# A chunk's and a state's products, put side by side on TensorE in the SSD part of a hybrid decoder layer

## The chip, the cores and the metric

The kernel runs on one core of a Trainium2 chip. The metric is the device time of one execution in microseconds. Three runs of the kernel before took 2318.2, 2318.97 and 2319.44 us; their median, 2318.97, is the time before.

## The reference

One inference step of a decoder layer: half a SwiGLU step, a mixer, half a SwiGLU step, each with a residual sum and an RMS norm ahead of it, and a last norm. 1024 positions of a prompt and 8 samples with 4 positions each go through the same weights (1056 columns in all). The mixer projects into two groups of heads, S5 and SSD. The change touches the SSD group: 24 heads of 64 in 4 groups of B and C, state of 128, chunks of 128 positions.

```python
acum = jnp.cumsum(la, axis=2)                       # la = dt * a, inside a chunk
decay = jnp.exp(jnp.where(mask, diff, -jnp.inf))    # diff[l, s] = acum[l] - acum[s]
cb = jnp.einsum('bclgn,bcsgn->bclsg', cm, bm)
y_diag = jnp.einsum('bclsg,bclsgr,bcsgrp->bclgrp', cb, decay, xd)
states = jnp.einsum('bclgn,bclgr,bclgrp->bcgrpn', bm, dstate, xd)
def step(hc, inp):
    st, dec = inp
    return hc * dec[..., None, None] + st, hc       # h_enter: the state ahead of each chunk
y_off = jnp.einsum('bclgn,bcgrpn,bclgr->bclgrp', cm, h_enter, jnp.exp(acum))
ys = (y_diag + y_off + d * xh) * silu(z)            # then a grouped RMS norm over 384 channels
```

The prompt has 8 chunks that hand a state on. Each of the 8 samples brings a state of its own (`h0`) into one short chunk of 4 positions; all 8 samples' positions lie in one block of 32 columns, called chunk 8 in the kernel.

## The kernel before

All heavy products are done with fp32 values split into two halves, so that a product is three matmuls: high by high, high by low, low by high. The 1056 columns are cut into three blocks of 352. `dense` (L301) runs over blocks and contraction tiles; one step of it, a `unit`, is the three matmuls of L317, L318 and L319 on one block, and after it `tick` (L192) is called.

**The order of the work is written out by ticks.** Whatever lies beside the dense products is put into queues with `later(gap, fn, q)` (L189). At every tick, `tick` issues the stores and the calls that `at(n, fn)` has set for this tick, then steps each queue: the first entry runs when at least `gap` ticks have passed since the queue's last step. An entry may be a generator; each `yield n` puts its rest back with gap n. Engines execute their own instructions in the order in which this program issues them, and wait for each other by semaphores. So a gap sets after how many dense units the instructions stand in each engine's queue, and not when they run.

**The SSD part** lies beside dense products: group 0 beside the projections of group 1 (`group(g)`, L1373, 8 tiles of 24 units), group 1 beside those of group 2, and so on; group 3 runs beside the output projections (`out`, L2020). `ssd_steps(g)` (L1700) gives `steps`, which queues nine rounds, i = 0 to 8, for chunks in the order 8, 0, 1, ..., 7:

- `stage_a(c)` (L1723). VectorE and ScalarE make the decay matrices (`dec`), ScalarE `ce`; after `a_dec` and `a_exp` ticks TensorE makes C by B and the transposes of B and x (L1743 to L1746), and the sums of the squares of an earlier chunk (`y_sums`, L1788); after `a_pe` VectorE makes `xd` and `xds`; after `a_mul` VectorE multiplies `dec`, and GpSimd `ce`.
- `stage_b(c)` (L1792), one round behind `stage_a`. TensorE makes the chunk's output into one bank (L1802: 12 products, 64 columns of stationary each, two of which lie side by side; 6 for chunk 0) and the new state into another (L1803). After `b_pe` VectorE adds the state up (`hT`) and GpSimd decays it (`hS`); after `b_y`, `y_done` (L1772) has VectorE make the gated output `yf`, ScalarE its square, and GpSimd two sums over the three channel tiles. The sums over the partitions are left to the next `y_sums`.
- `sample_h(b)` (L1839), the work on sample b's state: the store of the state before, the load of the state two ahead (after `sample` ticks), six products of the state (L1847, 64 columns of stationary and 4 streamed), one product for its update (L1848, 128 columns of stationary, 384 streamed), GpSimd's decay of the state, and after `add` ticks VectorE's two sums. `sample_b` (L1823) makes the output of the samples' block itself (L1828, once for a group, in round 1).

`sample_done` (L1860) ends a group: the sums of the last `y_done`, then the samples' `y_done`, then its sums. The last chunk's `stage_b(7)`, its sums and the row of norms are `tail` steps in round 0 of the next group. Four PSUM banks go round for these steps (`abank`, L246): two in `stage_a`, two in `stage_b`, one in `sample_h`. Buffers of `stage_a` (`prod`) are two deep, `xb` and the states three, `yf` one.

The gaps are in `GAP` (L36). Before the change a round is: `a` ticks, `stage_a`, `b` ticks, `stage_b`, `h` ticks, `sample_h`, with 4, 2 and 4 (in group 3: 4, 2 and 8), `first` and `second` in place of `a` in rounds 0 and 1.

Of the kernel before, what the change touches and what calls it, by code (L numbers as in the profile page):

```python
# [33 lines left out]
ADD, SUB, MUL = ALU.add, ALU.subtract, ALU.mult  # L34

GAP = dict(  # L36
    rs=14, rs1=1, rs2=1, a=4, b=2, h=4, a3=4, b3=2, h3=8, first=7, second=6, tail0=4, tail1=10, tail2=5, done=6, done2=6, done3=6, done4=6, add=4,
    a_dec=1, a_exp=2, a_pe=2, a_mul=2, b_pe=2, b_y=1, load_a=3, sample=6, split=18, split2=18, split_hi=5, split_lo=2, v0=1,
    v1=6, v2=6, v3=3, glu1=5, glu2=11, low=5, load=14, t0=12, t1=16, u0=8, u1=12, v_0=7, v_1=14, out=16, zout=2, s5z=6, row=4, s5a=6,
    s5b=5, s5c=6, s5d=4, prep=8, tiny=7, table=4,  # L40
# [94 lines left out]
class Build:  # L135
# [1564 lines left out]
    def ssd_steps(self, g):  # L1700
        nc, L, o = self.nc, self.later, self.o
# [70 lines left out]
        def y_done(c, n, x, z, p3, s):  # L1772
            cs = slice(128 * c, 128 * c + n)
            y = self.yf[:, :, 0:n]
            for j in range(3):
                self.stt(y[:, j], x[:, j], self.dcol[:, 3 * g + j:3 * g + j + 1], p3[:, j], MUL, ADD)
            self.tt(y, y, z, MUL)
            self.act(s, y, AF.Square)
            self.store(self.dO[g, :, :, cs].rearrange("j p c -> p j c"), y)
            for j in (1, 2):  # L1780
                self.tt(s[:, 0], s[:, 0], s[:, j], ADD, nc.gpsimd)
            cur["sum"] = (c, n, s[:, 0])

        def y_sums(p):

            if "sum" in cur:
                c, n, s = cur.pop("sum")
                nc.tensor.matmul(p[0:n, 400:401], s, self.ones[:, 0:1], start=True, stop=True)  # L1788
                return lambda: self.ts(self.rv[0:n, c:c + 1], p[0:n, 400:401], 1.0 / 384, MUL, EPS, ADD)
            return lambda: None  # L1790

        def stage_b(c):  # L1792
            xb, (dec, ce, xd, xds, bt) = cur.pop(c)
            z = cur.pop(("z", c))
            p3, p4 = self.abank(), self.abank()
            for j in range(3):
                for off in range(2 if c else 1):
                    for e in range(2):
                        out = p3[64 * e:64 * e + 64, 128 * j:128 * j + 128]
                        r = 2 * j + e  # L1800
                        lhs, rhs = ((xd, dec), (self.hT, ce))[off]
                        nc.tensor.matmul(out, lhs[:, 64 * r:64 * r + 64], rhs[:, r], start=(off == 0), stop=(off == 1 or c == 0))  # L1802
            nc.tensor.matmul(p4[:, 0:384], bt, xds, start=True, stop=True)  # L1803
            yield GAP["b_pe"]
            if c == 0:
                nc.vector.tensor_copy(self.hT, p4[:, 0:384])
            else:
                self.tt(self.hT, self.hS, p4[:, 0:384], ADD)
            if c < 7:
                self.tt(v6(self.hS), v6(self.hT), self.cd[:, c + 1, h6, None].broadcast_to([128, 6, 64]), MUL, nc.gpsimd)  # L1810
            yield GAP["b_y"]
            y_done(c, 128, xb[:, 2:5], z, p3[:, 0:384].rearrange("p (j c) -> p j c", j=3), xd.rearrange("p (j c) -> p j c", j=3))
            self.xb.put(xb)
            self.zg.put(z)
            if c == 7:
                nc.sync.dma_start(o["ssdp"][g], self.hT)

        def sample_load(b):
            h0 = self.h0.get()
            nc.sync.dma_start(h0, self.a["h0"][g, :, b])  # L1820
            cur["h", b] = h0

        def sample_b():  # L1823
            _, (dec, ce, xd, xds, bt) = cur.pop(8)
            p3 = self.abank()
            for r in range(6):
                out = p3[64 * (r % 2):64 * (r % 2) + 64, 32 * (r // 2):32 * (r // 2) + 32]
                nc.tensor.matmul(out, xd[0:32, 64 * r:64 * r + 64], dec[0:32, r, 0:32], start=True, stop=True)  # L1828
            nc.vector.tensor_copy(self.ys, p3[:, 0:96].rearrange("p (j c) -> p j c", j=3))

        def sample_m(b):
            self.ts(self.bm[b % 2], self.bst.bitcast(F32), self.bmask[:, b:b + 1], MUL)

        def sample_out(b):
            h0 = cur.pop(("h", b))
            nc.sync.dma_start(o["ssds"][g, :, b], h0)
            self.h0.put(h0)

        def sample_h(b):  # L1839
            h0, bm, p = cur["h", b], self.bm[b % 2], self.abank()  # L1840
            if b:
                sample_out(b - 1)
            if b + 2 < 8:
                self.at(GAP["sample"], lambda: sample_load(b + 2))
            for r in range(6):
                out = p[64 * (r % 2):64 * (r % 2) + 64, 384 + 4 * (r // 2):388 + 4 * (r // 2)]
                nc.tensor.matmul(out, h0[:, 64 * r:64 * r + 64], self.ces[:, r, 4 * b:4 * b + 4], start=True, stop=True)  # L1847
            nc.tensor.matmul(p[:, 0:384], bm, self.xst, start=True, stop=True)  # L1848
            self.tt(v6(h0), v6(h0), self.cds[:, b, h6, None].broadcast_to([128, 6, 64]), MUL, nc.gpsimd)

            def add():
                y = self.ys[:, :, 4 * b:4 * b + 4]
                self.tt(y, y, p[:, 384:396].rearrange("p (j c) -> p j c", j=3), ADD)
                self.tt(h0, h0, p[:, 0:384], ADD)
                if b < 7:
                    sample_m(b + 1)

            self.at(GAP["add"], add)
# [15 lines left out]
        def steps(nxt=None):  # L1874

            tail, self.tail = self.tail, [
                lambda: stage_b(7),
                lambda: (y_sums(self.abank())(), self.rs_root(self.ry))[1],
                lambda: (self.rs_row(self.ry, self.rsd[2 + g]), self.rs_done.add(g)),
            ]  # L1880
            ga, gb, gh = (GAP[k + ("3" if g == 3 else "")] for k in "abh")
            for i in range(9):
                c = (i + 8) % 9
                L((GAP["first"], GAP["second"])[i] if i < 2 else ga, lambda c=c: stage_a(c))
                if i == 0:
                    for n, fn in enumerate(tail):
                        L(GAP[f"tail{n}"], fn)
                    L(0, lambda: (load_z(8), load_z(0), sample_load(0), sample_load(1), sample_m(0)))
                else:
                    L(gb, sample_b if i == 1 else lambda c=c: stage_b(c - 1))  # L1890
                    if c < 7:
                        L(0, lambda c=c: self.at(6, lambda: load_z(c + 1)))
                    L(gh, lambda b=i - 1: sample_h(b))
            if nxt:
                L(0, nxt)
            L(GAP["done3" if g == 3 else "done"], sample_done)
# [255 lines left out]
```

## Time and profile before

| what | value |
|---|---|
| median of three runs | 2318.97 us |
| the profiled execution | 2322.18 us |
| its span, first to last instruction | 2320.5 us |
| mean granted TensorE clock | 0.993 |
| TensorE matmuls busy | 2277.6 us (98%), 16463 instructions |
| VectorE busy | 1509.0 us (65%) |
| ScalarE busy | 844.0 us (36%) |
| GpSimd busy | 383.0 us (17%) |
| SSD steps in the span | about 947 to 1523 us |

The page gives shares over the whole span, of which the SSD steps take a quarter. The lists in order of time carry the start in us from the span's start, the length, the engine, the line, what is written and read, how many instructions of that kind follow one another, and in square brackets the idle time of the engine ahead of it with what ended it. An fp32 product counts as two matmuls there. PEld is the load of stationaries, which can run under a matmul of the stationary before. Starts of matmuls are what to read; their lengths are modelled and overlap. In the view by stretches each engine has its busy time and number of instructions, then the granted clock, the DMA engines' share and GB/s.

### The profile page before, as it was taken

To read this page: it belongs to the slowest core of one execution; us is meant where nothing else is said; L and a number is where in the kernel's file an instruction comes from. 1 tells how busy PE (TensorE), PEld (TensorE's weight loads), DVE (VectorE), ACT (ScalarE), POOL (GpSimd) and SP (SyncE) were. 2 spreads that over 40 slices of the span, in tenths; PEclk is the share of its full clock that TensorE was granted. 3 is DMA by queue.
4 is the path that set the end of the run, shared out by engine and by line. 5 is a ranking of instruction groups with operands and counts; after the bars stand their busy time and mean duration, and the time that the engine had idled before them with its cause. 6 is when DMAs were issued, how large, how long until landed. Compare 5 with 4: busy or idle time off the path is not lost. (4 is left out here: it accounts for less than half of the span.)

```text
span 2320.5 us, 40946 instructions
## 1 busy us (share of the span) xinstructions
PE 2277.6 (98%) x16463; PEld 2218.2 (96%) x16463; DVE 1509.0 (65%) x3110; ACT 844.0 (36%) x1372; POOL 383.0 (17%) x446
## 2 busy tenths in 40 slices
PE   9999999999999999999999999999999999999997
PEld 9999999999999899999999889999999999999997
DVE  6988887662326377787889788767855555553325
ACT  5433334340113123555555553233433333341122
POOL 1200000000002133242333374422100000000013
PEclk9999999999999999999999999999999999999999
DMA  4222233362311354563555735432222222263112
GB/s 148 84 70 89 102 119 102 120 236 89 102 53 50 118 180 146 154 194 124 173 159 162 226 111 153 145 118 93 87 77 77 74 84 79 85 246 120 61 51 75
DMA packets 191548, 274.68 MB, mean 118 GB/s; under 512 B 31615, under 2 KB 137342, under 8 KB 191358
## 3 DMA queue, kind: packets, MB, share of 16 engines
q1 hardware_dynamic: 190782, 271.54, 35.7%
q8 instruction: 129, 2.11, 0.4%
q10 hardware_dynamic: 576, 0.52, 0.1%
q14 instruction: 61, 0.50, 0.1%
HBM read 195.17 MB, written 76.84 MB: 117 GB/s over the span
## 5 line engine op out<-in xcount | busy, mean ns | idle before, releaser
L317 PE MATMUL b<-xn,ws 128*128 128x352 f32 (+3 forms) x1776 | 595.0, 335 | 5.7 <-DVE tb L145 3.2
L318 PE MATMUL b<-xn,ws 128*128 128x352 f32 (+3 forms) x1776 | 574.9, 324 | 2.3 <-DVE xn L155 2.3
L319 PE MATMUL b<-xn,ws 128*128 128x352 f32 (+3 forms) x1776 | 574.1, 323 | 0.0
L317 PEld LDWEIGHTS b<-xn,ws 128*128 128x128 f32 x1776 | 335.4, 189 | 16.1 <-DVE tb L145 4.1
L318 PEld LDWEIGHTS b<-xn,ws 128*128 128x128 f32 x1776 | 337.4, 190 | 7.1 <-DVE xn L155 2.8
L681 PE MATMUL b<-xn,ws 128*128 128x264 f32 x1184 | 338.3, 286 | 5.8 <-ACT g L158 5.8
L683 PE MATMUL b<-xn,ws 128*128 128x264 f32 x1184 | 339.2, 286 | 2.3 <-DVE ws L145 2.3
L682 PE MATMUL b<-xn,ws 128*128 128x264 f32 x1184 | 338.5, 286 | 0.0
L319 PEld LDWEIGHTS b<-xn,ws 128*128 128x128 f32 x1776 | 335.9, 189 | 0.0
L158 ACT ACTIVATE ws<-wr 128x512 fp32r<-128x512 f32 (+4 forms) x208 | 170.3, 821 | 316.9 <-PE b L318 282.4
L145 DVE TENSOR_TENSOR ws<-wr,ws 128x512 fp32r<-128x512 f32 (+4 forms) x208 | 221.8, 1067 | 80.2 <-ACT ws L158 79.7
L681 PE MATMUL b<-d,ws 128*128 128x264 f32 x888 | 252.9, 285 | 1.0 <-DVE g L145 1.0
L682 PE MATMUL b<-d,ws 128*128 128x264 f32 x888 | 252.9, 285 | 0.0
L683 PE MATMUL b<-d,ws 128*128 128x264 f32 x888 | 252.8, 285 | 0.0
L145 POOL TENSOR_TENSOR acc<-acc,g 128x400 f32<-128x400 f32 (+2 forms) x25 | 37.6, 1503 | 1197.9 <-ACT g L158 1197.6
L155 DVE SCALAR_TENSOR_TENSOR x<-b,x 128x352 f32<-128x352 f32 (+2 forms) x144 | 73.5, 522 | 246.7 <-PE b L319 246.6
L681 PEld LDWEIGHTS b<-xn,ws 128*128 128x128 f32 x1184 | 224.2, 189 | 7.8 <-ACT g L158 7.1
L145 DVE TENSOR_TENSOR g<-b,g 128x264 f32<-128x264 f32 (+1 forms) x311 | 134.1, 432 | 150.1 <-PE b L683 105.1
L683 PEld LDWEIGHTS b<-xn,ws 128*128 128x128 f32 x1184 | 223.9, 189 | 3.1 <-DVE ws L145 3.1
L682 PEld LDWEIGHTS b<-xn,ws 128*128 128x128 f32 x1184 | 223.6, 189 | 0.0
L317 PE MATMUL b<-d,ws 128*128 128x352 f32 (+2 forms) x534 | 172.6, 323 | 0.0
L319 PE MATMUL b<-d,ws 128*128 128x352 f32 (+2 forms) x534 | 172.0, 322 | 0.0
(343 smaller groups left out, 4270.8 us busy)
## 6 DMA issues: line engine op xcount, KB each, us to landing
wr<-in_gu SPq DMA_DIRECT2D x68, 512.0 KB
dH<-g SPq DMA_DIRECT2D x74, 264.0 KB
wr<-in_win SPq DMA_DIRECT2D x36, 512.0 KB
wr<-in_dn SPq DMA_DIRECT2D x32, 512.0 KB
d<-dH SPq DMA_DIRECT2D x24, 528.0 KB
abc<-dA SPq DMA_DIRECT2D x32, 384.0 KB
xn<-dH SPq DMA_DIRECT2D x20, 528.0 KB
dC<-acc SPq DMA_DIRECT2D x20, 528.0 KB
```

Of the source, the lines that this page charges most:

```text
L145: (eng or self.nc.vector).tensor_tensor(out, x, y, op=op)
L155: self.nc.vector.scalar_tensor_tensor(out, x, s, y, op0=op0, op1=op1)
L158: self.nc.scalar.activation(out, x, f, **k)
L317: nc.tensor.matmul(p, wh[:, kc], xh, start=(k == 0), stop=False)
L318: nc.tensor.matmul(p, wh[:, kc], xl, start=False, stop=False)
L319: nc.tensor.matmul(p, wl[:, kc], xh, start=False, stop=(k == K - 1))
L681: nc.tensor.matmul(q, wh, xh, start=(k == 0 and name in ("P1", "P2", "P5")), stop=False, skip_group_check=True)
L682: nc.tensor.matmul(q, wh, xl, start=False, stop=False, skip_group_check=True)
L683: nc.tensor.matmul(q, wl, xh, start=False, stop=(k == 3), skip_group_check=True)
```

## The change

`sample_h(b)` no longer has a step of its own after the chunk. It runs in the step of `stage_b`, immediately ahead of it, so that on TensorE L1847, L1848, L1802 and L1803 follow one another. In round 1 it runs behind `sample_b`. The gap `h` goes; half of it is given to `a` and half to `b` (4 and 2 become 6 and 4; in group 3, 4 and 2 become 8 and 6). `add`, `done` and the others stay.

```diff
 GAP = dict(
-    rs=14, rs1=1, rs2=1, a=4, b=2, h=4, a3=4, b3=2, h3=8, first=7, second=6, ...
+    rs=14, rs1=1, rs2=1, a=6, b=4, a3=8, b3=6, first=7, second=6, ...
@@ steps
-            ga, gb, gh = (GAP[k + ("3" if g == 3 else "")] for k in "abh")
+            ga, gb = (GAP[k + ("3" if g == 3 else "")] for k in "ab")
             for i in range(9):
                 c = (i + 8) % 9
                 L((GAP["first"], GAP["second"])[i] if i < 2 else ga, lambda c=c: stage_a(c))
...
                 else:
-                    L(gb, sample_b if i == 1 else lambda c=c: stage_b(c - 1))
+
+                    L(gb, lambda c=c, b=i - 1: (sample_h(b), stage_b(c - 1))[1] if b else (sample_b(), sample_h(b))[1])
                     if c < 7:
                         L(0, lambda c=c: self.at(6, lambda: load_z(c + 1)))
-                    L(gh, lambda b=i - 1: sample_h(b))
```

## Rows read from the trace of the kernel before

**Rows 1.** Busy time by stretch, group 0 beside group 1's projections.

```profile
947.00:1066.00 119.00, 117.87 (x898) 110.78 (x898) 97.52 (x225) 64.08 (x93) 45.10 (x58) 1.00 0.51 163
```

**Rows 2.** TensorE in order of time: a chunk, a state, the next stage_a.

```profile
1149.84 0.32 PE L319 MATMUL b<-xn,ws 128*128 128x352 f32 x1
1150.10 0.44 PE L1802 MATMUL b<-dec,xd 128*64 128x128 f32 x4
...
1152.47 0.32 PE L318 MATMUL b<-xn,ws 128*128 128x352 f32 x1
...
1155.51 0.32 PE L319 MATMUL b<-xn,ws 128*128 128x352 f32 x1
1155.76 0.52 PE L1847 MATMUL b<-ces,h 128*64 128x4 f32 x12
1156.21 0.44 PE L1848 MATMUL b<-xst,bm 96*128 96x384 f32 x1
1156.49 0.33 PE L317 MATMUL b<-xn,ws 128*128 128x352 f32 x1
...
1159.71 0.32 PE L319 MATMUL b<-xn,ws 128*128 128x352 f32 x1
1159.87 0.38 PE L1743 MATMUL b<-xb 128*128 128x128 f32 x2
```

**Rows 3.** TensorE in order of time: the samples' own products.

```profile
957.56 0.54 PE L1828 MATMUL b<-dec,xd 32*64 32x32 f32 x12
958.02 0.43 PE L317 MATMUL b<-xn,ws 128*128 128x352 f32 x1
958.29 0.32 PE L318 MATMUL b<-xn,ws 128*128 128x352 f32 x1
```

**Rows 4.** Who waited for whom, 950 to 1520 us: total, times, longest.

```profile
PE b L1788 <- POOL xd L145: 4.2, 4, 2.5
...
DVE h L145 <- POOL h L145: 9.5, 13, 2.0
```

**Rows 5.** Four engines in order of time: one chunk's y_done to its sums.

```profile
1156.85 0.85 DVE L155 SCALAR_TENSOR_TENSOR yf<-xb,dcol,b 128x128 f32<-128x128 f32 x3
...
1158.39 0.53 ACT L158 ACTIVATE xd<-yf 128x384 f32<-128x384 f32 x1 [1.39 <-DVE yf L145]
...
1158.99 1.00 POOL L145 TENSOR_TENSOR xd<-xd 128x128 f32<-128x128 f32 x2 [1.15 <-ACT xd L158]
...
1160.53 0.28 PE L1788 MATMUL b<-ones,xd 128*128 128x1 f32 x2
```

**Rows 6.** TensorE in order of time: first and last of stage_a's 24 sums.

```profile
979.03 0.38 PE L1788 MATMUL b<-ones,xd 128*128 128x1 f32 x2 [1.13 <-POOL xd L145]
...
1484.78 0.28 PE L1788 MATMUL b<-ones,xd 128*128 128x1 f32 x2
```

**Rows 7.** In order of time: sums in sample_done of groups 1, 2, 3.

```profile
1197.52 1.00 POOL L145 TENSOR_TENSOR xd<-xd 128x128 f32<-128x128 f32 x2 [1.56 <-ACT xd L158]
...
1200.37 0.28 PE L1788 MATMUL b<-ones,xd 128*128 128x1 f32 x2
...
1200.79 0.58 DVE L155 SCALAR_TENSOR_TENSOR yf<-xsm,dcol,ys 128x32 f32<-128x32 f32 x3
...
1342.11 0.38 PE L1788 MATMUL b<-ones,xd 128*128 128x1 f32 x2 [2.46 <-POOL xd L145]
...
1496.56 1.00 POOL L145 TENSOR_TENSOR xd<-xd 128x128 f32<-128x128 f32 x2 [1.17 <-ACT xd L158]
...
1499.26 0.28 PE L1788 MATMUL b<-ones,xd 128*128 128x1 f32 x2
```

**Rows 8.** In order of time: a chunk's state product and the xds product.

```profile
1178.83 0.91 PE L1803 MATMUL b<-xds,bt 128*128 128x384 f32 x2
...
1180.92 0.54 DVE L145 TENSOR_TENSOR xds<-b,dtd 128x384 f32<-128x384 f32 x1
```

**Rows 9.** Busy time by stretch: the 5 us behind a stop.

```profile
1342.00:1347.00 5.00, 4.89 (x20) 4.57 (x20) 3.69 (x12) 0.92 (x2) 4.02 (x8) 0.66 0.79 249
```

More of the change, by code (lines that the diff above doesn't have):

```diff
@@ L36 @@
 GAP = dict(
-    rs=14, rs1=1, rs2=1, a=4, b=2, h=4, a3=4, b3=2, h3=8, first=7, second=6, tail0=4, tail1=10, tail2=5, done=6, done2=6, done3=6, done4=6, add=4,
+    rs=14, rs1=1, rs2=1, a=6, b=4, a3=8, b3=6, first=7, second=6, tail0=4, tail1=10, tail2=5, done=6, done2=6, done3=6, done4=6, add=4,
     a_dec=1, a_exp=2, a_pe=2, a_mul=2, b_pe=2, b_y=1, load_a=3, sample=6, split=18, split2=18, split_hi=5, split_lo=2, v0=1,
```

## The prediction

> **What bounds the kernel now.** I read first the busy times by stretch of the part in which the SSD steps run beside dense products. TensorE is busy in 117.87 of 119 us there, VectorE in 97.52 of 119 (82%) [rows 1]: the end is set by how long TensorE's own stream is, plus the places where it stops. The reader is to see that removing work from VectorE, ScalarE or GpSimd gains nothing by itself. Second, TensorE's list in order of time, for the price of leaving the dense stream and coming back. Third, the list of who waits for whom, for the stops: TensorE's one repeated stop in this part is L1788, the sum of squares of a chunk (y_sums), which waits for GpSimd [rows 4]. Fourth, the chain that feeds L1788, and the margin it has.
>
> **Part 1: the merged excursions, on TensorE.** A dense matmul of 352 columns starts every 0.161 us (1159.71 to 1159.87, where the 128-column products of stage_a follow without a gap) [rows 2]. A chunk's products begin 0.26 us after the last dense start, so 0.10 late (1149.84 to 1150.10), and the state's 0.25 after, so 0.09 late (1155.51 to 1155.76) [rows 2]. Both begin with stationaries of 64 columns. The state's excursion ends with L1848, 128 columns wide, 384 streamed, and the dense stream resumes behind it 0.28 us later (1156.21 to 1156.49) with no further loss; the whole costs 1156.49 - 1155.51 - 0.16 = 0.82 us. The chunk's costs 1152.47 - 1149.84 - 2 x 0.16 = 2.31 us [rows 2]. Merged, in the new order, the 0.10 us at the chunk's entry disappears only if L1848 does not bring the same loss. But L1848 is a full-width product just like the dense one, and what follows it is again L1802 with 64 columns. The switch from full to half width is not removed; it is moved from "dense to L1802" to "L1848 to L1802". No row shows that pair. The bounds are a gain of 28 x 0.10 = 2.8 us (no loss behind L1848; 7 merged chunks in each of 4 groups) and a loss of 28 x 0.12 = 3.4 us (the longer stream of L1848, 0.44 us against 0.32 in the rows, drains before the next weights load). I take 0, since the nearest rows, two entries out of a full-width stream, both lose the same.
>
> The Trainium skill, page "TensorEngine Tiling (Array Packing)", section "Key Properties", says that changing the tiling mode drains TensorE, whereas another tile of the same mode does not. By that rule the new order has as many mode changes for each chunk as the old one, and the term is 0; by the entry rows alone it could be -2.8 us.
>
> The sample's own products (sample_b, L1828, also 64 columns) lie next to the first state's after the change. Today L1828 starts at 957.56, the dense stream returns at 958.02 and its second matmul only at 958.29, 0.10 over the pitch [rows 3], and the state pays 0.09 to enter. Without the return: 0.10 + 0.09 and about 0.06 of the tail between them, 0.25 us, four times: -1.0 us (0 to -1.3).
>
> **Part 2: what moves, and who is late next.** A unit is one step of the dense loop, three matmuls, 0.48 us. By the gaps, the cycle keeps its length: 4 + 7 + 2 + 3 + 4 = 20 units before, 6 + 7 + 4 + 3 = 20 after (24 and 24 in group 3). Inside it, seen from stage_a's products, the chunk's come 2 units later and the state's 5 earlier (in group 3, 4 later and 7 earlier). sample_done follows the last state by 6 units before and the last y_done by 6 after.
>
> *The sums in stage_a.* From y_done to the next y_sums lie 4 + 4 + 1 + 2 = 11 units and the state's excursion before, 5.31 + 0.82 = 6.1 us; after, 6 + 1 + 2 = 9 units, 4.35 us: 1.78 us less. In that time the chain must run: one chunk has the three VectorE products at 1156.85, ScalarE's square at 1158.39, GpSimd's two sums from 1158.99 for 1.00, so 3.1 us, and L1788 at 1160.53 with 0.54 to spare [rows 5]. The 1.78 are not all lost: between stage_a's last VectorE product and hT lie two units and the state's excursion more than before, so a VectorE that is behind has 1.78 us more to catch up before y_done, less what the two units bring it. I take 1.1 us of 1.78 as regained where VectorE is behind (bounds 0 and 1.78), so each margin shrinks by 0.7. Twenty-four stage_a's carry such sums; the first stops, 979.03 with 1.13 us idle, and the last starts 4.9 us after its GpSimd pair [rows 6]. Worked out for all 24 in the same way, margins are -1.4, -0.6, -0.3, -0.1 (the stops, with what the matmul spacing loses), then 0.5, 0.7, 1.0, 1.3, 1.5, 1.6, 1.6, 1.7, 2.2, and eleven above 2.6. Less 0.7: four stops grow by 0.7 and one of 0.2 comes, +3.0 us. Less 1.78: +7.1 and eight new ones of 4.6 in all, +11.7. If everything is regained and VectorE's 9.5 us of waits for GpSimd's product of the state [rows 4], which now starts 5 units earlier with GpSimd idle, go too, the stops end: -2.4. I take +3.0.
>
> *The sums in sample_done.* From the last chunk's products to the first y_sums: 3 + 4 + 6 = 13 units and 0.82, 7.1 us, before; 3 + 6 = 9 units, 4.35, after; in group 3, 17 units and 0.82 = 9.0 before and 4.35 after. So 2.8 us less, and 4.7 in group 3; of it VectorE regains as above 1.1 (group 3: some 1.9). Group 0 waits for the next group's convolution there (its last step has spare units), so it pays nothing. Group 1: GpSimd's pair ends at 1198.52, L1788 at 1200.37, margin 1.85 [rows 7]; less 1.7 to 2.8: 0 to 0.9, I take 0.3. Group 2 already stops 2.46 us [rows 7]; +1.7 to 2.8, I take 1.7. Group 3: margin 1499.26 - 1497.56 = 1.7 [rows 7], less 2.8 to 4.7: a new stop of 1.1 to 3.0, I take 2.0. Together +4.0 (0 to 6.7). Behind it the sample's y_done overwrites yf, whose store to HBM must have landed: today it starts at 1200.79 without waiting [rows 7], some 3.9 us after the product that is stored (which ends just before the square, 0.6 before GpSimd's pair as in [rows 5]); after the change some 2 us after it. VectorE may wait 0 to 2 us, the second y_sums 0 to 1.1 in three groups: I take +0.5 (0 to 3.3).
>
> *The banks.* Four banks serve five uses in a cycle. Before, the fifth (the state's) reused the bank of stage_a's transposes; after, the chunk's L1803 does, 6 units behind the product xds that reads it. Today xds can end 1181.46 against L1803 at 1178.83 [rows 8], 2.63 us later; L1803 moves 0.97 + 0.82 = 1.79 later, so it would stop 0.8 us there. Two more chunks exceed it (0.6 and 0.4). All that stands behind L1803 on TensorE is the dense stream. I take half of the 1.8, +0.9 (0 to 1.8), as a stop ahead of it gives VectorE the time. stage_a's first product now takes the bank of the state's sum, whose VectorE read stands right behind y_done: it is ready before L1788 is, so it adds nothing.
>
> *The clock.* After the stop of 2.46 us the granted clock of the following 5 us is 0.66 of full [rows 9], part of it at 1.2 GHz instead of 2.4: 0.34 x 5 = 1.7 us lost. Group 3's new stop, and a chunk's, come near that length. I take half of one, +0.8 (-3.2 if both of today's go, +3.2).
>
> *Moved at no cost.* The state's store and load on SP's queue, and its GpSimd product, go 5 units earlier; three state buffers and 16 units since the last VectorE sum cover the store, and the load still has 34 units. The load of the next chunk's inputs waits for y_done to free its buffer with 2 units less room; SP may stop 1.5 us with weights behind it, which are fetched a tile ahead.
>
> Sum: 0 - 1.0 + 3.0 + 4.0 + 0.5 + 0.9 + 0.8 = +8.2 us. The profiled execution took 2322.18 us (span 2320.5), 3.2 above the median of the three runs, 2318.97. On its own time the sum gives 2330.4; on the median, which is what I predict, 2327.2.
>
> **Rivals.**
> 1. *Nothing to see*: VectorE regains all of the 1.78, as it idles 18% of the time [rows 1]; only sample_done's stops grow by 2 to 4, less 1.0: 2318 to 2322, say 2320.5. Against: the conv taps are emitted by units, so the backlog at y_done returns.
> 2. *Faster*: one loss of entry for each merged pair is really gone, and the earlier GpSimd product frees VectorE, so L1788 stops waiting. It pays from the point at which the drain behind L1848 is hidden: -2.8 - 1.0 - 2.4 and one fall of the clock, -1.7: -7.9, 2311. For it: 9.5 us of VectorE waits. Against: L1848 is as wide as the dense product.
> 3. *Heavy stops*: VectorE regains nothing. 11.7 + 6.7 + 1.8 + 3.2 + 1 - 1.0 = +23, 2342. For it: the chain has 0.54 us in a usual chunk. Against: each stop gives VectorE its length back.
> The change might also not do what it says, since the full-width L1848 keeps the halves apart; that is the forecast's part 1 and not a case of its own.
>
> **How the numbers follow.** Forecast (+3 to +14) 0.50, rival 1 0.26, rival 2 0.14, rival 3 0.10. A measurement of this kernel can tell 0.2%, 4.6 us, from no change. Slower by more: 0.43 of the forecast and rival 3, 0.53. Within: 0.07 and most of rival 1, 0.32. Faster: 0.15. The range 2313 to 2336 leaves out the upper part of rival 3 and the lower of rival 2; the forecast's own is 2322 to 2333.
>
> **What would show it.** L1848 to L1802 at 0.37 us in TensorE's list confirms part 1; 0.28 refutes it. The waits of L1788 for xd should rise from 4.2 us to 11 to 13, with a new stop at group 3's sample_done, and L1803 should wait for VectorE's xds two or three times. If L1788's waits stay near 4, part 2 is wrong and rival 1 or 2 holds.

## The result, and the profile after

The changed kernel takes 2343.95 us (median of four runs, 2341.76 to 2344.37), the kernel before 2319.20 beside it: a ratio of 1.0101, 95% interval [1.0089, 1.0114]. The forecast was slower, 2327.2 with a range of 2313 to 2336. The direction was right, the size three times too small, and the result lies outside the range. The profiled execution took 2344.35 us (span 2342.6).

The page first. Each engine's busy time, share of the span and number of instructions:

```profile
PE 2284.2 (98%) x16463; PEld 2225.0 (95%) x16463; DVE 1510.0 (64%) x3110; ACT 847.0 (36%) x1373; POOL 395.6 (17%) x446
```

ScalarE has one instruction more, a table load (1372 before); the others have as many as before. GpSimd alone is busier by more than 10 us (383.0 before); since it does the same work, something slows it. Next the stretch of [rows 1], and the 5 us behind the longest stop of a sample's sums, as in [rows 9] (length, busy time and number for PE, PEld, DVE, ACT and POOL, then the granted clock, DMA share, GB/s):

```profile
947.00:1066.00 119.00, 114.67 (x866) 107.60 (x865) 96.75 (x221) 61.62 (x89) 48.02 (x58) 0.99 0.50 156
1354.30:1359.30 5.00, 5.00 (x22) 4.76 (x23) 2.70 (x8) 0.97 (x2) 3.12 (x5) 0.66 0.90 249
```

In the same 119 us TensorE is busy 3.2 us less: it stands still for longer. TensorE in order of time through a merged step (answers to [rows 2]) and through sample_b with the first state (answers to [rows 3]):

```profile
1144.32 0.32 PE L319 MATMUL b<-xn,ws 128*128 128x352 f32 x1
1144.57 0.52 PE L1847 MATMUL b<-ces,h 128*64 128x4 f32 x12
1145.02 0.44 PE L1848 MATMUL b<-xst,bm 96*128 96x384 f32 x1
1145.39 0.44 PE L1802 MATMUL b<-dec,xd 128*64 128x128 f32 x4
...
1147.31 0.62 PE L317 MATMUL b<-xn,ws 128*128 128x352 f32 x1
1147.76 0.32 PE L318 MATMUL b<-xn,ws 128*128 128x352 f32 x1
...
956.95 0.54 PE L1828 MATMUL b<-dec,xd 32*64 32x32 f32 x12
957.41 0.52 PE L1847 MATMUL b<-ces,h 128*64 128x4 f32 x12
957.86 0.44 PE L1848 MATMUL b<-xst,bm 96*128 96x384 f32 x1
958.14 0.32 PE L317 MATMUL b<-xn,ws 128*128 128x352 f32 x1
```

L1802 starts 0.37 us behind L1848, not 0.28. The merged step costs 1147.76 - 1144.32 - 2 x 0.16 = 3.12 us, exactly the 0.82 + 2.30 of the two apart: putting the products side by side saved nothing. Beside sample_b 0.2 us are saved, four times. So the loss is in waits. TensorE's waits for others (total us, times, longest), which answer to [rows 4]:

```profile
PE b L1788 <- POOL xd L145: 10.2, 8, 3.4
PE b L1743 <- DVE h L145: 6.0, 2, 3.1
PE b L1788 <- POOL raw L1323: 2.4, 2, 2.1
...
PE b L1803 <- DVE xds L145: 1.4, 2, 0.7
```

One such stop, with all the engines in order of time, where [rows 5] had 0.54 us to spare:

```profile
1133.15 0.86 DVE L155 SCALAR_TENSOR_TENSOR yf<-xb,dcol,b 128x128 f32<-128x128 f32 x3
...
1134.60 0.55 DVE L145 TENSOR_TENSOR h<-h,b 128x384 f32<-128x384 f32 x1
...
1134.70 0.53 ACT L158 ACTIVATE xd<-yf 128x384 f32<-128x384 f32 x1 [4.96 <-DVE ys L145]
1135.30 3.40 POOL L145 TENSOR_TENSOR xd<-xd 128x128 f32<-128x128 f32 x2 [1.15 <-ACT xd L158]
1135.69 0.86 DVE L155 SCALAR_TENSOR_TENSOR dec<-abc,acum,cmask 128x128 f32<-128x128 f32 x3
...
1138.76 0.38 PE L1788 MATMUL b<-ones,xd 128*128 128x1 f32 x2 [2.09 <-POOL raw L1323]
```

y_done, ScalarE's square, GpSimd's pair and L1788 follow as foreseen. (`raw`, which the view names at L1788, is a short fill of 0.10 us that GpSimd runs right behind the pair.) But GpSimd's pair takes 3.40 us, where [rows 5] had 1.00, with VectorE at the six `dec` and the taps of the convolution meanwhile. The state's add (`h`) stands right behind y_done.

I take a stop as the time from the last dense start to the second dense start behind it, less two pitches and less the least that this kind of step costs in the trace. Summed over the SSD part, before and after: stage_a 2.6 and 15.7; the sums in sample_done and tails 4.1 and 8.2; chunks 0.2 and 1.6; the row of norms (L403) 3.3 and 1.1; stops inside the dense stream (a start over 0.3 us late) 7.9 and 9.9; dense matmuls at a slower pitch 3.8 and 9.9. The 15.7 of stage_a hold both waits of the list above, that for the sums and that for `h`. With sample_b's -0.8 all this is about +24, and the kernel ahead of the SSD part was 1.5 faster in this execution; the spans differ by 22.1.

### The profile page after: what moved, and what is told of

The parts are those of the page before. It is cut to its first block, busy times and chain, and to the rows that moved or that the text cites. A ratio compares the mean times of both kernels' runs of the same rounds, so it can differ in the third digit from the quotient of the medians.

```text
span 2342.6 us, 40922 instructions
## 1 busy us (share of the span) xinstructions
PE 2284.2 (98%) x16463; PEld 2225.0 (95%) x16463; DVE 1510.0 (64%) x3110; ACT 847.0 (36%) x1373; POOL 395.6 (17%) x446
## 4 chain that ended last, share of the span: by engine, by line
PE 80%; DVE 10%; ACT 2%; issue 2%; DMA 2%; POOL 2%; SPq 1%; DVEq 0%; ACTq 0%; POOLq 0%
PE b L317 14%; PE b L318 14%; PE b L319 14%; PE b L681 9%; PE b L682 9%; PE b L683 9%; DVE x L145 2%; DVE ws L145 1%; PE b L1802 1%; PE b L346 1%; PE b L347 1%; PE b L348 1%; POOL xd L145 1%; DVE cacc L155 1%; PE b L1803 1%
## 5 line engine op out<-in xcount | busy, mean ns | idle before, releaser
L317 PE MATMUL b<-xn,ws 128*128 128x352 f32 (+3 forms) x1776 | 597.2, 336 | 5.0 <-DVE x L145 2.1
L317 PEld LDWEIGHTS b<-xn,ws 128*128 128x128 f32 x1776 | 338.0, 190 | 15.1 <-DVE x L145 3.4
L317 PE MATMUL b<-d,ws 128*128 128x352 f32 (+2 forms) x534 | 172.6, 323 | 0.0
```

The source lines that it names most:

```text
L317: nc.tensor.matmul(p, wh[:, kc], xh, start=(k == 0), stop=False)
```

## The experiments

Times are medians; a ratio is to the kernel before on the same chip. The column `units` below counts dense units from the start of group 1's projections, read from TensorE's order in the program: where sample_done of groups 1, 2 and 3 stands.

| kernel | units | ratio |
|---|---|---|
| before | 408, 617, 858 | 1 |
| changed | 406, 613, 850 | 1.0101 |
| f1_same_places | 412, 621, 862 | 1.0077 |
| g1_places_kept | 408, 617, 858 | 1.0020 |
| h1_stage_places_kept_done_short | 404, 609, 842 | 1.0119 |
| h2_after_without_drift | 408, 617, 858 | 1.0065 |
| h3_before_with_drift | 408, 615, 854 | 1.0071 |

**First: distance or adjacency?** Four versions, three of them of the changed kernel.

```diff
 e1_gaps_back, on the changed kernel
-a=6, b=4, a3=8, b3=6, second=6, done=6, done3=6
+a=8, b=2, a3=12, b3=2, second=8, done=10, done3=14
 e2_apart, on the kernel before
-a=4, b=2, h=4, a3=4, b3=2, h3=8
+a=6, b=4, h=0, a3=8, b3=6, h3=0
 e4_done_back, on the changed kernel
-done=6, done3=6
+done=10, done3=14
 e3_dec_behind, on the changed kernel (stage_a; a=9, a3=11, first=10, second=9)
+            # the load, L1743 to L1746 and y_sums first
             for r in range(6):
                 self.stt(dec[:, r], ...)
...
-            yield GAP["a_exp"]
-            # L1743 to L1746 and y_sums here
-            yield GAP["a_pe"]
+            yield 1
```

> The changed kernel, products still merged, but with the units given back to the place between y_done and the next sums: a=8, b=2 (group 3: 12 and 2), second=8, done=10 (group 3: 14). y_done to stage_a's sums is 11 units again, y_done to VectorE's dec 8, sample_done's sums 13 units behind the chunk (group 3: 17). Theories of where the 24.8 us of the change went: D (distance): the chain yf, square, GpSimd's two sums has 1.8 us less, and in stage_a that alone makes L1788 stop. G (GpSimd beside dec): the two GpSimd sums now run while VectorE makes the next dec, and last up to 4.9 us instead of 1.0 to 1.5; that makes most of the stops. A (adjacency): the merged products themselves, or the state's banks and buffers, cost. D and G expect 2316 to 2324 (ratio to before 0.998 to 1.002; the sample's merged products save 0.8 us). A expects 2335 or more.

2354.04 us, 1.0147 [1.0124, 1.017]. D and G miss by 30 us. The time lies in A's range, which has no upper end, but A is not tested by it: second=8 and the longer `done` moved groups 1 to 3 later (sample_done at 414, 625 and 868), and the last group's tail was cut: it takes 24 units behind the second sum of sample_done (unit 874), and begin(3), which forces the rest out at unit 888, left it 14.

> The kernel before, products not merged (the state behind y_done, with no unit between), but with the changed kernel's gaps: a=6, b=4, h=0 (group 3: 8, 6, 0). y_done to the sums is 9 units and the state's excursion of 0.82 us, 0.8 more than in the changed kernel and 1.0 less than before; dec comes 6 units behind y_done. A (adjacency) expects the time of before, 2317 to 2323. D and G expect most of the loss without any merging: D 2326 to 2336 (about half, as the distance lies half way), G 2330 to 2340 (dec still lies on the GpSimd sums).

2336.09 us, 1.0071 [1.0045, 1.0097]. The gaps without the merging cost two thirds of the loss, so the adjacency of the products is not its main cause. (Its groups end as early as those of the changed kernel; see below.)

> The changed kernel with the order inside stage_a turned: TensorE's transposes and sums first, 9 units behind y_done as in the changed kernel, and VectorE's six dec products behind them (3 units later than now); exp, xd and the dec product follow as before, closer together; the round keeps its length. So the distance from y_done to the sums is the same, and only VectorE's dec no longer lies in front of the sums. D expects no gain: 2340 to 2346. G expects the GpSimd pair back at 1.0 to 1.5 us in the six rounds where it took 1.9 to 4.9, so about 8 us of stops and 2 to 4 of clock less: 2330 to 2335.

2339.54 us, 1.0083 [1.0061, 1.0105], between the two expectations, and its interval overlaps the changed kernel's: open. The mean of GpSimd's sums fell from 748 to 602 ns (568 before).

> The changed kernel with only the gap ahead of sample_done as long as before the change in units behind the last chunk (done=10, group 3: 14). It tells sample_done's share of the loss: by the stops in the trace 4.1 us of L1788 (0.5 in group 1, 0.9 more in group 2, 1.1 in group 3, 1.8 in the tails) and up to one fall of the clock. Both D and G expect 2337 to 2343; under A no change, 2341 to 2346.

2359.07 us, 1.0168 [1.0147, 1.019]. A miss for all three theories: with sample_done's distance alone restored the time is longer. The groups then end later than in the kernel before, each by more than the one ahead of it (414, 625, 870).

**Second: places kept, and the chain itself.**

```diff
 f1_same_places, on the changed kernel
-a=6, b=4, a3=8, b3=6, done=6, done3=6
+a=8, b=2, a3=12, b3=2, done=10, done3=14
 f2_same_places_wide_first: f1, and in sample_h
+            if b:
+                nc.tensor.matmul(p[:, 0:384], bm, self.xst, ...)
             for r in range(6): ...            # L1847
-            nc.tensor.matmul(p[:, 0:384], bm, self.xst, ...)
+            if not b:
+                nc.tensor.matmul(p[:, 0:384], bm, self.xst, ...)
 f3_before_two_earlier, on the kernel before
-first=7, done=6, done3=6
+first=5, done=8, done3=8
 f4_sums_on_tensor, on the changed kernel
-            for j in (1, 2):                  # y_done
-                self.tt(s[:, 0], s[:, 0], s[:, j], ADD, nc.gpsimd)
...
-                nc.tensor.matmul(p[0:n, 400:401], s, self.ones[:, 0:1], start=True, stop=True)
+                for j in range(3):            # y_sums
+                    nc.tensor.matmul(p[0:n, 400:401], s[:, j], self.ones[:, 0:1], start=j == 0, stop=j == 2)
```

> The changed kernel with gaps that put every unit of stage_a, stage_b, sample_done and the group's tail back on the dense unit that it has in the kernel before (a=8, b=2, a3=12, b3=2, done=10, done3=14, second=6); only the state's products keep their new place in front of the chunk's. The earlier try at this had second=8 and ran two units longer per group, so that mix_out's begin(3) forced the rest out. Theory distance (the sums of y come 9 units behind y_done instead of 11 and the sample's sums 6 instead of 10; that is the whole cost): 2316 to 2323 us, stops of L1788 and L1743 in stage_a under 4 us in sum. Rival adjacency (state and chunk side by side, the adds of h queued right behind y_done on VectorE, the bank of the state's sum met by stage_a's L1743): 2330 to 2345, L1743<-DVE h still 5 us or more.

2337.23 us, 1.0077 [1.006, 1.0095]. The time lies in the rival's range, but neither case was tested: group 0's end waits for the convolution, so ten gaps instead of six made groups 1 to 3 four units later (table above).

> f1_same_places with L1848 (the full-width product) ahead of the six 64-column L1847 for b over 0, so that L1847 and L1802, both of 64 columns, follow one another and TensorE changes its width twice in the merged step instead of four times. If a change of width costs about 0.1 us each, as the excursions' enter and exit show, 28 merged steps cost 5 to 8 us less on TensorE: f1's time less 5 to 8, 2310 to 2317 under the distance theory. Rival (the cost is in the products, not in the change of width): equal to f1 within 2 us, merged step still 3.12 us.

2334.03 us, 1.0063 [1.0048, 1.0078]. The merged step fell to 2.82 us as expected. The median fell by 3 us and not by 8, and the two intervals overlap; in the traces the stops are longer than in f1 (stage_a 14.0 and 16.7 us, merged steps 2.2 and 4.0).

> The kernel before with every unit of a group's SSD part two dense units earlier (first=5) and the last sample's step where it was (done=8, done3=8): distances within a round are those of the kernel before, only the sample's first sums get two units more. Only the place against the steps of the convolution and of S5 is another. Theory distance: 2315 to 2320 us (nothing but up to 4 us less at the sample's sums). Rival place (what counts is which steps of the other queue meet y_done on VectorE and GpSimd, and any shift costs): 2324 to 2340, with new stops of L1788 in stage_a.

2321.32 us, 1.0005 [0.9996, 1.0015]: 1.3 us above the first range, under the rival's, and not told apart from the kernel before. The experiment is weaker than its text: done=8 gave the units back, and only group 0's rounds moved.

> The changed kernel with GpSimd's two additions of y_done left out and y_sums as three accumulating L1788 (one per 128 rows) instead of one: the hop over GpSimd, 1.0 us alone and up to 4.9 us beside VectorE's stream, is gone from the chain of the sums; TensorE gets 72 products of one column more (24 to 36 rounds, about 0.06 us each: +4 us or less). Theory distance with GpSimd's lengthening as its size: stops of L1788 fall from 12.6 us to under 4, L1743<-DVE h stays, in all 2334 to 2340 us. Rival (VectorE alone is late, GpSimd only follows): stops fall by no more than 1 us per stop, and the time is 2343 to 2349.

2338.84 us, 1.0085 [1.007, 1.01]: the first expectation, in time and in stops. The three products cost 0.44 us more in each of 24 sums and 0.26 in each of 12, 13.7 us, not 4; the median is still 5 us under the changed kernel's, though the two intervals overlap. TensorE's waits:

```profile
PE b L1743 <- DVE h L145: 6.7, 4, 2.9
...
PE b L1787 <- ACT xsm L158: 1.6, 2, 1.1
...
PE b L1787 <- ACT xd L158: 0.6, 2, 0.4
```

The 12.6 us behind GpSimd (10.2 and the 2.4 under `raw`) are 2.2 behind ScalarE (the sums are L1787 here), so GpSimd's hop carries most of that wait. stage_a's stops, 15.7 us above the least, are 9.6 above the least of this kernel. The 6 us of L1743 behind the state's add stay, at the same two places: there it is not the hop that comes last.

**Third: the merging alone, with every unit as before.**

```diff
 g1_places_kept, on the changed kernel
-a=6, b=4, a3=8, b3=6
+a=8, b=2, a3=12, b3=2
-            L(GAP["done3" if g == 3 else "done"], sample_done)
+            L((6, 10, 10, 14)[g], sample_done)
 b1_after_old_banks, on the changed kernel
+        def merged(c, b):
+            p3, p4, p = self.abank(), self.abank(), self.abank()
+            sample_h(b, p)
+            return stage_b(c - 1, (p3, p4))
 g3_only_products: g1 and b1, and in sample_h all but the products goes
+            self.at(GAP["add"] * (1 + (g == 3)) + (3 if b else 0), rest)
 g4_only_products_wide_first: g3, and the order of f2
```

> The changed kernel with stage_a, stage_b, sample_done and the tails on the dense units of the kernel before in every group: a=8, b=2, a3=12, b3=2 and sample_done 6, 10, 10 and 14 units behind the last chunk (f1_same_places gave group 0 ten too, where the wait for the convolution had taken up the state's four units already, and so ran four units late from there on). ScalarE's program is then the same as before; what is still moved is the state's step: its products, GpSimd's h and VectorE's two adds and bm, which stand right behind y_done instead of seven units later. Theory distance (only y_done's distance to the sums and to the sample's sums costs): 2316 to 2323 us, stops of L1788 and L1743 as before, under 5 us. Rival queue (the adds behind y_done, GpSimd's h ahead of its pair of sums, and the bank that L1743 takes cost by themselves): 2325 to 2334, with L1743<-DVE h over 3 us.

2323.25 us, 1.0020 [1.0011, 1.0029]; span 2320.5, that of the kernel before. TensorE's waits:

```profile
PE b L1788 <- POOL xd L145: 5.3, 4, 1.8
PE b L1803 <- DVE xds L145: 3.7, 3, 1.5
```

Four fifths of the loss are gone with the products still side by side. What stays, 0.2%, lies between the two expectations. L1743 waits for `h` once, 0.3 us.

> The kernel before in all but TensorE's order: the state's products stand in front of the chunk's, and GpSimd's h, VectorE's adds, the loads and stores of the state and the banks stay where they were (the rest of sample_h runs 7 units later, 11 in the last group). Theory distance and rival queue both: the merging itself costs nothing, 2315 to 2320 us (0.8 us saved beside sample_b). Rival adjacency on TensorE (the 3.1 us excursion in one piece lets the dense stream's producers or the clock suffer): 2324 or more, with the granted clock under 0.992.

2358.22 us, 1.0161 [1.0146, 1.0176]. The first range is missed by 38 us. The rival of adjacency has no upper end and so contains the time (and the clock, 0.991), but the loss is not in the adjacency: one wait makes most of it:

```profile
PE b L1844 <- DVE xds L145: 28.5, 14, 4.2
```

L1844 is L1847 in this kernel. With the third bank for the state, the step's first product takes the bank from which VectorE's `xds` of four units ago still reads.

> g3_only_products with L1848 ahead of L1847, so that the 64-column products of the state and of the chunk follow one another. The merged step measured 2.82 us with this order and 3.12 without; 28 of them make 8.3 us. If nothing is given back, 2307 to 2312 us, faster than the kernel before by 7 to 11 us; if every stretch that TensorE gains is given back in stops of L1788 (the producers of the sums are late by as much), 2314 to 2319.

2357.54 us, 1.0162 [1.0148, 1.0176], with the same wait (29.4 us): a miss of both cases.

> The changed kernel with the banks of accumulation in the order of the kernel before (the chunk's two first, then the state's), all places as in the changed kernel. L1743 then waits for the reader of y's bank and no longer for the state's adds. Theory: the 6.0 us of L1743<-DVE h go, some of them back to L1788 which stands behind them: 2338 to 2342 us. Rival (the bank is no bound, what is late is the same VectorE queue): 2342 to 2346.

2353.3 us, 1.0145 [1.0129, 1.0161], above both ranges. L1743's wait for `h` went, and 8.0 us of waits for `xds` at the step's start came (L1848 is L1847 here):

```profile
PE b L1788 <- POOL xd L145: 12.0, 10, 2.0
PE b L1848 <- DVE xds L145: 8.0, 6, 3.0
```

In the changed kernel's own order of banks this wait stands at L1803, the step's last product, 2.3 us later. The stops in stage_a did not go with the wait for `h`: they are 15.4 us here and 15.7 in the changed kernel. Where L1743 no longer waits for the add, L1788 behind it waits for the sums.

**Fourth: what of g1 can be mended, and which distance counts.**

```diff
 g2_places_kept_wide_first: g1 and the order of f2
 g5_products_first_bank_wide_first: g2, and the rest of sample_h later as in g3
 h1_stage_places_kept_done_short, on the changed kernel
-a=6, b=4, a3=8, b3=6
+a=8, b=2, a3=12, b3=2
```

> g1_places_kept (2323.3 us) with L1848 ahead of L1847: 28 merged steps at 2.82 us instead of 3.12, 8.3 us less on TensorE. If the stops stay as in g1_places_kept: 2313 to 2317 us, faster than the kernel before by 2 to 6. If the shorter step is given back in stops, because VectorE and GpSimd need the time and not TensorE: 2319 to 2324.

2318.42 us beside 2320.66, 0.9992 [0.9983, 1.0001]: between the two expectations and not told apart from the kernel before. Against g1 the order of widths is worth 0.28%, about 6.5 us of the 8.3. The merged step, L1846 being L1848 and L1849 being L1847:

```profile
1147.93 0.32 PE L319 MATMUL b<-xn,ws 128*128 128x352 f32 x1
1148.09 0.34 PE L1846 MATMUL b<-xst,bm 96*128 96x384 f32 x1
1148.37 0.52 PE L1849 MATMUL b<-ces,h 128*64 128x4 f32 x12
1148.74 0.42 PE L1802 MATMUL b<-dec,xd 128*64 128x128 f32 x4
```

L1846 follows the dense product at the dense pitch, and the step changes from 128 to 64 columns once instead of twice. The Trainium skill, page "TensorEngine Tiling (Array Packing)", section "Key Properties", says that a change of mode drains TensorE; the trace agrees, at 0.30 us for one change to 64 columns and back.

> g4_only_products_wide_first with the state's sum in the first of the round's three banks, as in the changed kernel, so that L1848 no longer waits for this round's xds; VectorE's, GpSimd's and ScalarE's programs stay those of the kernel before. The 29.4 us of L1843<-DVE xds go and nothing takes their place but L1743, whose bank the state's adds give back about 4 units ahead of it: 2309 to 2314 us, the fastest so far. Rival (the adds are late for L1743): 2318 to 2330, with L1743<-DVE h over 5 us.

2342.61 us, 1.0102 [1.0086, 1.0117]. The rival's wait came, four times over, and the time is 12 us above its range:

```profile
PE b L1743 <- DVE h L145: 22.4, 12, 4.7
```

With the state's adds in their old place, seven units later, L1743 finds its bank unread twelve times. The changed order of banks needs the adds to come early.

> The changed kernel with a=8, b=2, a3=12, b3=2 and sample_done still 6 units behind the last chunk: stage_a's sums have the distance that they have in the kernel before, the sample's sums the short one of the changed kernel. Theory stage (most of the cost is the 24 sums in stage_a, which stopped TensorE 13 us more): 2325 to 2331 us. Theory sample (the four sample_done carry most): 2335 to 2343.

2347.84 us, 1.0119 [1.0105, 1.0132]. Neither theory. Stops in stage_a fell from 15.7 to 4.2 us as they should, but others came, of which no distance had changed against g1:

```profile
PE b L1803 <- DVE xds L145: 13.0, 5, 4.4
```

g1 and h1 differ in where groups 2 and 3 stand, and in sample_done's distance. The second is no part of the way to L1803, and four of the five waits lie in groups 2 and 3; that their place makes these stops is argued, not shown.

**Fifth: distance without drift, drift without distance.**

```diff
 h2_after_without_drift, on the changed kernel
-            L(GAP["done3" if g == 3 else "done"], sample_done)
+            L((6, 8, 8, 10)[g], sample_done)
 h3_before_with_drift, on the kernel before
-                L((GAP["first"], GAP["second"])[i] if i < 2 else ga, ...)
+                L(((7, 7, 5, 5)[g], GAP["second"])[i] if i < 2 else ga, ...)
```

> The changed kernel with sample_done 6, 8, 8 and 10 units behind the last chunk instead of 6 each. In the changed kernel a group is 2 dense units shorter than before (4 in the last), so that its groups 2 and 3 begin 2 and 4 units earlier against the convolution than in the kernel before; here every stage_a, sample_done and tail has its unit of the kernel before, and only the chunk and y_done come 2 units later and the state 5 units earlier. Theory distance (y_done to the sums 9 units instead of 11 is the cost): 2338 to 2344 us. Rival drift (the cost is that the groups' steps meet others of the convolution's on VectorE): 2324 to 2332.

2335.27 us, 1.0065 [1.005, 1.008], between the two.

> The kernel before with first=5 instead of 7 in groups 2 and 3: these groups then stand 2 and 4 units earlier against the convolution, as in the changed kernel, and all distances within a group are those of the kernel before. (f3_before_two_earlier moved group 0 alone, since its done=8 gave the units back.) Theory distance: 2317 to 2322 us. Rival drift: 2328 to 2340, with new stops in groups 2 and 3.

2337.02 us, 1.0071 [1.0058, 1.0084]: the rival. TensorE's waits, of h2 and then of h3:

```profile
PE b L1788 <- POOL xd L145: 10.1, 7, 3.4
PE b L1743 <- DVE h L145: 5.2, 2, 3.2
```

```profile
PE b L1788 <- POOL xd L145: 6.2, 4, 2.2
PE b L317 <- ACT xn L158: 5.1, 1, 5.1
PE b L1803 <- DVE h L145: 4.6, 4, 2.2
```

h2 has the changed kernel's waits for the sums and its bank, almost unchanged. h3 has a stop of 5 us in the dense stream and stops of chunks behind VectorE's adds, at unchanged distances. What ends that stop, in the kernel before, in h3, and in the changed kernel:

```profile
1504.56 2.43 POOL L145 TENSOR_TENSOR raw<-raw,rs 128x1056 f32<-128x1056 f32 x1
1512.72 1.46 POOL L145 TENSOR_TENSOR xd<-xd 128x128 f32<-128x128 f32 x2 [5.73 <-ACT xd L158]
```

```profile
1517.14 0.98 POOL L145 TENSOR_TENSOR xd<-xd 128x128 f32<-128x128 f32 x2 [6.62 <-ACT xd L158]
1518.08 2.40 POOL L145 TENSOR_TENSOR raw<-raw,rs 128x1056 f32<-128x1056 f32 x1
1520.52 1.17 ACT L158 ACTIVATE xn<-raw,wn 128x1056 fp32r<-128x1056 f32 x1 [3.46 <-POOL raw L145]
1521.74 0.66 PE L317 MATMUL b<-xn,ws 128*128 128x352 f32 x1 [5.07 <-ACT xn L158]
```

```profile
1522.92 0.53 ACT L158 ACTIVATE xd<-yf 128x384 f32<-128x384 f32 x1 [8.51 <-DVE yf L145]
1523.35 1.16 ACT L158 ACTIVATE xn<-cacc,wn 128x1056 fp32r<-128x1056 f32 x1
1528.07 0.43 PE L318 MATMUL b<-xn,ws 128*128 128x352 f32 x1 [2.66 <-DVE xn L155]
```

`cacc` and `raw` are the input of the next projection, which GpSimd multiplies by the row of norms (`rs`) and ScalarE and VectorE then split into halves (`xn`). In the kernel before GpSimd makes `raw` ahead of the last chunk's pair of sums. In h3, four units earlier, the pair stands ahead of `raw` in GpSimd's queue and waits 6.62 us for its square; `raw`, ScalarE's half of the split and TensorE's L317 wait behind it. In the changed kernel, whose last group ends eight units earlier, the last chunk's square stands ahead of both splits on ScalarE and waits 8.51 us for `yf`, and TensorE stops for 2.66 us (1.53 at this place before).

**Last: VectorE's order alone.**

```diff
 g7_wide_first_dec_behind: g2, and in stage_a (a=11, a3=15, first=10, second=9)
+            # the load, L1743 to L1746, y_sums, then after a_pe xd, done() and xds
             for r in range(6):
                 self.stt(dec[:, r], ...)      # the rest follows
...
-            yield GAP["a_exp"]
+            yield 1
```

> g2_places_kept_wide_first (2318.4 us) with stage_a's products and sums first and its six dec behind xd and xds (a=11, a3=15, first=10, second=9; every unit of TensorE's steps as in g2). VectorE's burst of dec then no longer runs beside GpSimd's pair of sums and no longer stands ahead of xds, for which L1803 waits 4.9 us and behind which L1788 waits 5.6 us in g2. Theory (these two waits are what is left of the change's price): 2311 to 2316 us, faster than the kernel before. Rival (another step of VectorE takes their place, dec now comes late for its own product): 2318 to 2326.

2350.86 us, 1.0135 [1.0118, 1.0152]. The rival, and much heavier than it said, with every TensorE step on g2's unit. GpSimd's sums took 598 ns on the mean (655 in g2), and TensorE stopped more. At one place on VectorE `dec` waits for ScalarE's exponential, with hT and y_done queued behind it; how much of the 32 us over g2 this makes is not shown.

```profile
1018.46 0.95 DVE L145 TENSOR_TENSOR dec<-dec,b 128x768 f32<-128x768 f32 x1 [0.91 <-ACT dec L158]
...
1021.42 0.54 DVE L145 TENSOR_TENSOR hT<-hS,b 128x384 f32<-128x384 f32 x1
```

## Why the prediction was wrong

**Part 1 was right.** Merging saved 0.0 us in a chunk's step and 0.8 in all at sample_b (forecast 0 and -1.0), and L1848 to L1802 took the 0.37 us that was to confirm it.

**The sums in stage_a were mis-sized.** Forecast +3.0, bounds -2.4 and +11.7; measured +13.1, and +17.1 in h2, where nothing drifts. The step that failed is "each margin shrinks by 0.7". From a chunk's last L1802 to stage_a the mean time fell by 2.1 us (2.7 in group 3, for which the text took 1.78 as well). From that L1802 to the first `yf` it fell from 4.32 to 3.26: 1.1 us regained, as forecast. But GpSimd's pair grew from 1.18 to 1.68 on the mean, and so the mean margin fell by 1.5, from 2.0 to 0.5. Two things were wrong in it.

First, the chain behind y_done was taken as fixed ("GpSimd's two sums from 1158.99 for 1.00"). With `dec` two units and the state's excursion nearer, the pair took 3.4 us and, once, 4.9; its mean went from 568 to 748 ns per sum. Six of the nine stops, 8.0 us, stand behind a pair of 1.7 us or more. The kernel before has two pairs of 2.2 us, so its trace could have told. f4, which takes the hop out, left 2.2 of the 12.6 us of L1788's waits. That the pair's length alone makes these six is not shown: e3 shortened it and gained at most 4 us, and g7 had it short and was slow.

Second, the time regained did not go to the sums that were latest. The two longest stops, 3.6 and 3.5 us, stand behind pairs of 1.45 and 0.99 us. Their `yf` starts 6.13 and 8.23 us behind the last L1802, where it started 6.17 and 8.47 before. In one of the two VectorE is busy with the convolution's taps; in the other it stands idle, 6.02 us before and 7.58 after, since `tb`, made from a result of the dense stream, is ahead of hT and y_done in its queue and waits for its own inputs. That one, before (first line) and after:

```profile
1319.83 0.53 DVE L145 TENSOR_TENSOR tb<-b,rs 128x352 f32<-128x352 f32 x1 [6.02 <-DMA rs<-rsd]
1332.09 0.52 DVE L145 TENSOR_TENSOR tb<-b,rs 128x352 f32<-128x352 f32 x1 [7.58 <-PE b L319]
1334.38 0.85 DVE L155 SCALAR_TENSOR_TENSOR yf<-xb,dcol,b 128x128 f32<-128x128 f32 x3
1336.54 0.99 POOL L145 TENSOR_TENSOR xd<-xd 128x128 f32<-128x128 f32 x2 [1.40 <-ACT xd L158]
1336.85 0.49 PE L1743 MATMUL b<-xb 128*128 128x128 f32 x2 [2.94 <-DVE h L145]
1337.61 0.36 PE L1788 MATMUL b<-ones,xd 128*128 128x1 f32 x2
```

**"It adds nothing" was nearly right.** In the list of waits the bank of the state's sum has 6.0 us, all at these two stops. But here the pair ends at 1337.53, and L1788 follows at once: without the bank it would have waited until then. At the other stop the pair ends 0.2 us ahead of the add, and L1788 comes 1.0 us behind the pair. So of the 6.0 some 1 us is the bank's, and b1, without that wait, stops for 2.7 and 3.7 us there. L1788's waits for GpSimd, 12.6 us, lie in the 11 to 13 that the text named as its sign; the stops of the sums that stand under L1743 come on top.

**A term was missing: the drift.** The prediction counted that a round keeps its 20 units, and that sample_done follows the last y_done by 6. It did not draw the consequence: a group ends two units earlier (four in the last), the next begins so, and groups 2 and 3 stand 2 and 4 units earlier against the convolution and the splits. In the kernel before that costs 0.71%, some 16 us (h3). In the changed kernel it costs less: merging alone, every stage's place kept, is 0.20% (g1, 4.6 us, with the state's adds early); merging and distances are 0.65% (h2), so the distances make some 10; the whole is 1.01%, so some 8 us are left for the drift, and for sample_done's shorter distance, which h2 does not have in full. Added in another order the parts come out otherwise, as the 16 of h3 shows. The dense stream bears it out: its stops and its slower pitch together are 11.7 us before, 10.2 in h2, 19.8 in the changed kernel and 19.8 in h3.

**sample_done** came to +4.1 with the tails (forecast +4.5), but its own stop of group 2 grew by 0.9 and not by 1.7, and a tail carries 1.3. **Banks** at L1803: +1.4 (forecast +0.9, bound 1.8). **The clock**: +6.1, the slower pitch, against +0.8. Behind a stop of 3.4 us the 5 us are granted 0.66 again, as in [rows 9]. In the SSD part the granted clock is at its lower level, half of full, twice before, 6.8 us in all, and six times after, 23.9 us; it was their number that was missed.

Two readings are to be set right. L1788 was not TensorE's one repeated stop before: its list of waits also has two of L317 for `tb`, 3.2 us. The eight new stops add up to 4.3 us by the margins given, not to 4.6.

Rival 3 named the right size, 2342, for partly the wrong reason: VectorE did regain its time on the mean, and regained nothing where the two longest stops are.

## What to carry to other kernels

Where an order is written by hand, list where each step stands before and after, to the end of the stream, and not only within a round: two units that a group loses move everything behind it against the other queue. Take the length of a step in a chain from a round in which its neighbours run beside it, and read for the tightest margins themselves what the engine waits for: a mean regain says nothing of them. When products of different tile widths are put together, set equal widths side by side: that, not the adjacency, was worth 0.30 us of TensorE's time a step.

## What the runs showed of the hardware

- GpSimd's two sums of 128x128 take 1.00 us alone [rows 5] and 3.40 beside VectorE's stream of products with two inputs in SBUF; in the kernel before two pairs already took longer, 2.19 and 2.20, of which one is:

```profile
1251.92 2.20 POOL L145 TENSOR_TENSOR xd<-xd 128x128 f32<-128x128 f32 x2 [1.32 <-ACT xd L158]
```

The Trainium skill, page "SBUF — State Buffer", section "SBUF: two separate sides", says that VectorE with two inputs in SBUF and GpSimd take turns at one port pair, each for a whole instruction. The trace agrees in direction: three times the length, not a fixed price.

- One change from 128 columns to 64 and back costs TensorE 0.30 us between full streams (3.12 against 2.82, over 24 steps).
- A sum over partitions with one streamed column costs TensorE's dense stream 0.22 us as one product and 0.48 as three that accumulate (12 sums of f4, the least of each); behind stage_a's transposes the two more cost 0.44.
